# Layer-0 attention with the queries on partitions: a scan over the keys in place of triangular products

## The chip, the cores and the metric

The kernel runs on one core of a Trainium2 chip. The core has five instruction queues: TensorE (PE in the profile; its weight loads are a row of their own, PEld), VectorE (DVE), ScalarE (ACT), GpSimd (POOL) and SyncE (SP, which here issues the weight loads). Each queue runs its instructions in a fixed order; an instruction waits on semaphores for what it reads and for the buffer that it overwrites. The metric is the device time of one execution in microseconds (us); lower is better.

## What is computed

A trunk of two decoder layers over 256 tokens of 1024 features. Layer 0 is stick-breaking attention with 16 heads of 64, then an MLP with squared ReLU; layer 1 is a sparse attention with three branches and a second MLP. Only the attention of layer 0 is touched:

```python
z = jnp.einsum('bqhd,bshd->bhqs', q_blk, k).astype(jnp.float32) * scale
causal = key_pos[None, :] < t[:, None]
log_1m = jnp.where(causal, jax.nn.log_sigmoid(-z), 0.0)
excl = lax.cumsum(log_1m, axis=3, reverse=True) - log_1m
a = jnp.where(causal, jnp.exp(jax.nn.log_sigmoid(z) + excl), 0.0)
return jnp.einsum('bhqs,bshd->bqhd', a.astype(v.dtype), v)
```

With softplus(z) = ln(1 + exp z), log_sigmoid(-z) is -softplus(z) and log_sigmoid(z) is z - softplus(z). So the weight of a key is the exponential of z minus the sum of softplus over this key and all later keys that the query may see. Masked keys count zero in the sum and have weight zero.

## The kernel before

**Weights.** All weights stream through SBUF in pieces of 1 MB in the order of their use. `fetch` (L69) loads a piece on SP, `split` (L79) makes two halves of it: ACT copies a half to `wh` in the reduced format that TensorE multiplies in (L89), DVE subtracts to get the rest, `wl` (L90). Three pieces of each kind fit. Every product with a weight is then three matmuls (`mm3`, L124 to L127): high by high, high by low, low by high. `step` (L100) puts the splitting of a later piece between the matmuls of the present one.

**Attention of layer 0** (`layer0`, L289) works on pairs of heads, p = 0 to 7. Each pair has one row of a piece of `wqk` and goes through four stages:

- `proj(p)` (L345): 48 matmuls of 256 columns give the transposed queries and keys; one DVE multiplication, `qkT` (L354), scales them by the norm of each token.
- `scores(p)` (L357): keys on partitions, queries along the row. Three blocks of 128 x 128 per head: keys 0-127 with all queries, keys 128-255 with the later queries. Two more matmuls add the mask as a bf16 matrix to the diagonal blocks. Softplus is then made on ACT and DVE: absolute value, exponential, logarithm (L373 to L375), and max(z, 0) added (L377). The result is split in two, `sbh` on ACT (L381) and `sbl` on DVE (L382).
- `suffix(p)` (L385): the sum over later keys runs across partitions, so TensorE makes it: products with a triangle of -1 (`tri`) are added to the scores in PSUM, for both parts and both heads, eight matmuls in all. ACT takes the exponential, `sba` (L393), which is the attention weight with keys on partitions, as the next product wants it.
- `values(p)` (L396): weights times values into `po`; `o_evac` (L197) splits the result into `oT_h` on ACT (L198) and `oT_l` on DVE (L199).

The loop (L407 to L414) runs `suffix(p)`, `scores(p+1)`, `values(p)`, `proj(p+2)`. The output projection (`out_proj`, L208) follows, 96 matmuls of 512 columns; the last pair's `suffix` and `values` are hung into it.

**Order of the work.** A planner orders the instructions of each engine when the program is built. In general it follows the order of the program among those that it reckons to be ready; where it reckons a wait, later work moves ahead (the scores of pair 0 stand inside `proj(1)`). Once built, the order is fixed whatever the real durations are.

**PSUM.** Eight banks under two names: four `a` (products of weights, `po`) and four `z` (scores and others). A pair's two score banks are held from `scores` until its exponential in `suffix` has been read, about one period of the loop.

Of the kernel before, what the change touches and what calls it, by code (L numbers as in the profile page):

```python
# [7 lines left out]
F32 = mybir.dt.float32  # L8
# [23 lines left out]
C_ID, C_SB, C_CA, C_TRI, C_ONE, C_CM, C_ANY, C_COS, C_SIN, C_BLK, C_PW, C_END = (  # L32
    0, 128, 256, 384, 512, 640, 670, 672, 704, 736, 740, 744)
# [3 lines left out]
def hybrid_kernel(ctx, tc, x, eye, gcols, gfin, wqk, wv, wo0, wkv, wqa, wqb, wqc, wo1, w1, w2, cw1, cw2, cpos, gate_b, consts, out):  # L37
# [21 lines left out]
    # the weights in the order of their use: loaded ahead, split in two exact parts  # L59
# [19 lines left out]
    def split():  # L79
        """the next half of a piece, split"""  # L80
        j, half = divmod(parts[0], 2)
        parts[0] += 1
        n = stream[j][1]
        if half == 0:
            made.append((wp.tile([P, n], F32R, tag="wh", name="wh", bufs=3),
                         wp.tile([P, n], F32R, tag="wl", name="wl", bufs=3)))
        r = slice(half * n // 2, (half + 1) * n // 2)
        h, lo = made[j]
        nc.scalar.copy(h[:, r], raws[j][:, r])  # L89
        nc.vector.tensor_sub(lo[:, r], raws[j][:, r], f32(h[:, r]))  # L90
        if half:
            fetch()
# [56 lines left out]
    cbf = cp.tile([P, 3 * P], BF16, name="cbf")  # L149
    ident_b, sbm_b, cam_b = cbf[:, 0:P], cbf[:, P:2 * P], cbf[:, 2 * P:3 * P]  # L150
    tri = cp.tile([P, 2 * P], F32R, name="tri")
# [4 lines left out]
    def var_of(parts_):  # L156
        """mean of squares plus eps, per token"""
        ss = sp.tile([P, 2], F32, name="ss")
        for i, src in enumerate(parts_):
            sq = sp.tile([P, D], F32, name="sq", tag="y")  # L160
            tc.keep_in_program_order(
                nc.scalar.activation(sq[:, 0:src.shape[1]], src, AF.Square, accum_out=ss[:, i:i + 1]))
        v = sp.tile([P, 1], F32, name="v", bufs=4)
        if len(parts_) == 2:
            nc.vector.tensor_add(ss[:, 0:1], ss[:, 0:1], ss[:, 1:2])
        nc.vector.tensor_scalar(v, ss[:, 0:1], 1.0 / D, EPS, op0=OP.mult, op1=OP.add)
        return v
# [6 lines left out]
    def xt_tr(half):  # L174
        """four feature blocks of the residual stream, transposed; even blocks in one bank, odd ones in the other"""
        pt = [bank2(f"pt{b}").rearrange("p (j q) -> p j q", j=2) for b in range(2)]
        for b in range(2):
            for j in range(2):
                k = 4 * half + 2 * j + b
                for t in range(T):  # L180
                    nc.tensor.transpose(pt[b][:, j, t * P:(t + 1) * P], hres[t][:, k * P:(k + 1) * P], ident)
        return pt

    def xt_evac(pt, half, gi, xt):
        """times the gain of each feature, split in two"""
# [41 lines left out]
    def mlp(layer, gi, xt, mid, ap):  # L227
        """xt holds the first half of the blocks already; mid runs inside the last products"""
# [60 lines left out]
    def layer0(ap):  # L289
# [33 lines left out]
        nc.gpsimd.tensor_copy(cbf, cst[:, 0:3 * P])  # L323
        nc.gpsimd.tensor_copy(tri, cst[:, C_TRI:C_TRI + 2 * P])
# [32 lines left out]
        def scores(p):  # L357
            qkT = live[p]
            qT, kT = qkT[:, 0, :], qkT[:, 1, :]
            z = [bank2(f"z{hd}") for hd in range(2)]  # L360
            mb = sbm_b[:, None, :].to_broadcast([P, 2, P])
            for hd in range(2):
                r = slice(hd * DH, (hd + 1) * DH)
                mm(z[hd][:, 0:256], kT[r, 0:P], qT[r, :], True, False)
            for hd in range(2):
                r = slice(hd * DH, (hd + 1) * DH)
                mm(z[hd][:, 256:384], kT[r, P:2 * P], qT[r, P:2 * P], False, False)
            for hd in range(2):
                zd = z[hd][:, 0:512].rearrange("p (a q) -> p a q", a=2)[:, :, 0:P]
                mm(zd, ident_b, mb, False, False)  # L370
            na = ap.tile([P, 2, 384], F32, name="na")
            for hd in range(2):
                nc.scalar.activation(na[:, hd, :], z[hd][:, 0:384], AF.Abs)  # L373
            nc.scalar.activation(na, na, AF.Exp, scale=-1.0)
            nc.scalar.activation(na, na, AF.Ln, bias=1.0)  # L375
            for hd in range(2):
                nc.vector.scalar_tensor_tensor(na[:, hd, :], z[hd][:, 0:384], 0.0, na[:, hd, :],  # L377
                                               op0=OP.max, op1=OP.add)
            sh = ap.tile([P, 2, 384], F32R, name="sbh")
            sl = ap.tile([P, 2, 384], F32R, name="sbl")  # L380
            nc.scalar.copy(sh, na)  # L381
            nc.vector.tensor_sub(sl, na, f32(sh))  # L382
            live[p] = z, sh, sl

        def suffix(p):  # L385
            z, sh, sl = live[p]
            for i, a in enumerate((sh, sl)):
                for hd in range(2):
                    mm(z[hd][:, 0:384], tri[:, 0:P], a[:, hd, :], False, False)
                    mm(z[hd][:, P:2 * P], tri[:, P:2 * P], a[:, hd, 256:384], False, i == 1)  # L390
            a = ap.tile([P, 2, 384], F32, name="sba")
            for hd in range(2):
                nc.scalar.activation(a[:, hd, :], z[hd][:, 0:384], AF.Exp)  # L393
            live[p] = a

        def values(p):  # L396
            a = live.pop(p)
            po = bank2("po") if p == NP - 1 else bank("po")
# [11 lines left out]
        for p in range(NP - 1):  # L410
            suffix(p)
            scores(p + 1)
            values(p)
            if p + 2 < NP:  # L414
                proj(p + 2)
        xn = xt_tiles("n")
        out_proj(oT, i_o0, {(0, 0, 3): [lambda: suffix(NP - 1)], (0, 1, 0): [lambda: values(NP - 1)],
# [3 lines left out]
    def nsa(xk, pt0, ap):  # L421
# [47 lines left out]
        def rope(src, t, n):  # L469
            """src[:, h, 0:16] rotated in place; sin holds (-sin, sin), cos (cos, cos)."""  # L470
# [10 lines left out]
        # compressed blocks: windows of the transposed keys and values, plus positions  # L481
# [32 lines left out]
        # keys of the selected and window branches: rotated, transposed, on either half of the partitions, split  # L514
# [37 lines left out]
        # compressed keys and values  # L552
# [114 lines left out]
        # compressed branch: probabilities times gates, transposed, for heads 8 * hf .. 8 * hf + 7  # L667
# [36 lines left out]
        # selected and window branches, and the gated sum of all three  # L704
# [158 lines left out]
def _constants():  # L863
# [4 lines left out]
    c[:, C_SB:C_SB + P] = np.where(i[:, None] < i[None, :], 0.0, NEG)  # L868
    c[:, C_CA:C_CA + P] = np.where(i[None, :] <= i[:, None], 0.0, NEG)
    c[:, C_TRI:C_TRI + P] = np.where(i[:, None] >= i[None, :], -1.0, 0.0)  # L870
    c[:, C_ONE:C_ONE + P] = -1.0
# [17 lines left out]
def _layout(inp):  # L889
# [6 lines left out]
    def blocks(w, nk, cw):  # L896
        """[K, N] -> [N / cw, K / (nk * 128), 128, nk * cw]"""
# [49 lines left out]
```

## Time and profile before

| | us |
|---|---|
| median of 3 runs | 657.2 |
| lowest and highest run | 655.12, 657.46 |
| span of the profiled execution, first to last instruction | 654.1 |
| PE busy | 640.1 (98%) |
| DVE busy | 397.3 (61%) |
| ACT busy | 352.2 (54%) |
| POOL busy | 57.9 (9%) |
| mean granted TensorE clock (share of full speed) | 0.998 |

The profiled execution has its span on record, but no time of its own; the median of the runs is 3.1 us above the span. Times within the trace are counted from the start of the span. Layer 0's attention proper, from the first `qk` product to the first `pu` product of the MLP, runs from 31.3 to 130.1 us. Matmuls are pipelined: one record lasts longer than the distance to the next, so what a matmul costs PE is read from start to start.

### The profile page before, as it was taken

To read this page: it belongs to the slowest core of one execution; us is meant where nothing else is said; L and a number is where in the kernel's file an instruction comes from. 1 tells how busy PE (TensorE), PEld (TensorE's weight loads), DVE (VectorE), ACT (ScalarE), POOL (GpSimd) and SP (SyncE) were. 2 spreads that over 40 slices of the span, in tenths; PEclk is the share of its full clock that TensorE was granted. 3 is DMA by queue.
4 is the path that set the end of the run, shared out by engine and by line. 5 is a ranking of instruction groups with operands and counts; after the bars stand their busy time and mean duration, and the time that the engine had idled before them with its cause. 6 is when DMAs were issued, how large, how long until landed. Compare 5 with 4: busy or idle time off the path is not lost.

```text
span 654.1 us, 10023 instructions
## 1 busy us (share of the span) xinstructions
PE 640.1 (98%) x4096; PEld 563.6 (86%) x4096; DVE 397.3 (61%) x558; ACT 352.2 (54%) x588; POOL 57.9 (9%) x91
## 2 busy tenths in 40 slices
PE   8999999999999999999999999999999999999995
PEld 5899887899999998988888987767998989999994
DVE  5665554675454545555899888773765555454544
ACT  5776676364444444444866767662464454444433
POOL 1000000000000000000133334550000000000000
PEclk9999999999999999999999999999999999999999
DMA  8853332545555554555545750101555555555501
GB/s 325 299 181 126 128 97 98 174 147 193 194 193 194 178 196 164 198 171 187 202 156 177 264 191 2 66 1 63 178 195 180 194 189 193 192 193 193 178 18 64
DMA packets 16894, 106.87 MB, mean 163 GB/s; under 512 B 2256, under 2 KB 2512, under 8 KB 4944
## 3 DMA queue, kind: packets, MB, share of 16 engines
q1 hardware_dynamic: 15696, 104.92, 45.5%
q10 hardware_dynamic: 1152, 1.31, 0.7%
q8 instruction: 32, 0.52, 0.3%
q14 instruction: 14, 0.11, 0.0%
HBM read 105.17 MB, written 1.05 MB: 162 GB/s over the span
## 4 chain that ended last, share of the span: by engine, by line
PE 87%; ACT 4%; DVE 4%; DMA 2%; POOL 2%; issue 1%; SPq 0%; POOLq 0%; ACTq 0%; DVEq 0%
PE acc L125 11%; PE acc L126 11%; PE acc L127 11%; PE pu L126 9%; PE pu L127 9%; PE pu L125 9%; PE po L130 4%; PE qk L125 2%; PE qk L126 2%; ACT wh L89 2%; PE qk L127 2%; PE z L130 2%; PE pk L127 2%; PE pk L126 2%; PE pk L125 2%
## 5 line engine op out<-in xcount | busy, mean ns | idle before, releaser
L90 DVE TENSOR_TENSOR wl<-raw,wh 128x1024 fp32r<-128x1024 f32 (+3 forms) x202 | 237.6, 1200 | 181.5 <-ACT wh L89 181.1
L89 ACT CAST wh<-raw 128x1024 fp32r<-128x1024 f32 (+3 forms) x202 | 200.3, 1023 | 213.1 <-issue 103.8
L126 PE MATMUL pu<-xln,wh 128*128 128x256 f32 x512 | 145.0, 283 | 0.0
L127 PE MATMUL pu<-xhn,wl 128*128 128x256 f32 x512 | 144.9, 283 | 0.0
L125 PE MATMUL pu<-xhn,wh 128*128 128x256 f32 x512 | 144.5, 283 | 0.0
L125 PE MATMUL acc<-wh,hh 128*128 128x512 f32 x256 | 100.0, 392 | 0.0
L126 PE MATMUL acc<-wl,hh 128*128 128x512 f32 x256 | 99.7, 391 | 0.0
L126 PEld LDWEIGHTS pu<-xln,wh 128*128 128x128 f32 x512 | 98.1, 192 | 1.4 <-DVE xln L191 0.2
L127 PE MATMUL acc<-wh,hl 128*128 128x512 f32 x256 | 99.2, 389 | 0.0
L125 PEld LDWEIGHTS pu<-xhn,wh 128*128 128x128 f32 x512 | 98.0, 192 | 1.2
L127 PEld LDWEIGHTS pu<-xhn,wl 128*128 128x128 f32 x512 | 98.1, 192 | 0.0
L127 PEld LDWEIGHTS acc<-wh,hl 128*128 128x128 f32 x256 | 48.1, 188 | 10.5 <-DVE hl L269 0.2
L125 PEld LDWEIGHTS acc<-wh,hh 128*128 128x128 f32 x256 | 48.2, 188 | 9.6 <-ACT hh L268 0.5
L126 PEld LDWEIGHTS acc<-wl,hh 128*128 128x128 f32 x256 | 48.2, 188 | 8.8
L125 PE MATMUL qk<-xha,wh 128*128 128x256 f32 x128 | 36.8, 288 | 0.0
L127 PE MATMUL qk<-xha,wl 128*128 128x256 f32 x128 | 36.3, 283 | 0.0
L126 PE MATMUL qk<-xla,wh 128*128 128x256 f32 x128 | 36.2, 283 | 0.0
L739 POOL TENSOR_TENSOR pe<-pe,rs 128x256 f32<-128x256 f32 (+1 forms) x32 | 26.2, 841 | 25.5 <-DVE rs L735 19.8
L268 ACT CAST hh<-ms 128x512 fp32r<-128x512 f32 x32 | 19.9, 622 | 14.6 <-DVE ms L264 14.6
L699 POOL MEMSET kcb<- 128x120 f32 x1 | 0.2, 200 | 291.1 <-PE acc L127 291.1
L125 PE MATMUL acc<-wh,oT_h 128*128 128x512 f32 x64 | 25.6, 400 | 0.0
L125 PEld LDWEIGHTS qk<-xha,wh 128*128 128x128 f32 x128 | 24.5, 191 | 1.1 <-issue 1.0
(188 smaller groups left out, 972.3 us busy)
## 6 DMA issues: line engine op xcount, KB each, us to landing
raw<-in_w SPq DMA_DIRECT2D x64, 1024.0 KB, 4.8
raw<-in_wqk SPq DMA_DIRECT2D x8, 1024.0 KB, 4.9
raw<-in_wo SPq DMA_DIRECT2D x8, 1024.0 KB, 4.8
raw<-in_wkv SPq DMA_DIRECT2D x6, 1024.0 KB, 5.0
raw<-in_cw SPq DMA_DIRECT2D x4, 1024.0 KB, 5.1
raw<-in_wv SPq DMA_DIRECT2D x3, 1024.0 KB, 7.1
raw<-in_wqb SPq DMA_DIRECT2D x2, 768.0 KB, 4.2
raw<-in_wqc SPq DMA_DIRECT2D x2, 768.0 KB, 5.2
```

What stands on the lines that cost most here:

```text
L89: nc.scalar.copy(h[:, r], raws[j][:, r])
L90: nc.vector.tensor_sub(lo[:, r], raws[j][:, r], f32(h[:, r]))
L125: nc.tensor.matmul(o, a[0], b[0], start=first, stop=False, skip_group_check=True)
L126: nc.tensor.matmul(o, a[0], b[1], start=False, stop=False, skip_group_check=True)
L127: nc.tensor.matmul(o, a[1], b[0], start=False, stop=last, skip_group_check=True)
L130: nc.tensor.matmul(o, a, b, start=first, stop=last, skip_group_check=True)
L268: nc.scalar.copy(hh, sv)
L699: nc.gpsimd.memset(kcb, 0.0)
L739: nc.gpsimd.tensor_tensor(s, s, rs[:, t, :][:, :, None].to_broadcast([P, 2, n]), op=OP.mult)
```

## The change

The scores are made with the queries on partitions and the keys along the row. The sum over later keys is then a sum along the row, which one DVE instruction, a scan from the last key to the first, makes for both heads at once. The row of a head has three segments of 128 scores, each followed by one column that holds -1e30 (`SEG` = 129, `ROW` = 387). The factor `go_on` is 1 except at two such columns, where it is 0 and restarts the sum.

The mask is a minimum with a constant, 40 or -1e30, taken by DVE when it reads the scores out of PSUM. Softplus is made directly as ln(1 + exp z), so the absolute value, the maximum and the split in two are gone. The weights come out with queries on partitions and have to be turned: a new stage `turn(p)` transposes six blocks on TensorE and copies them out of PSUM, one head on ACT and one on DVE. The loop runs one pair further ahead: the scores of pair p+2 are made while pair p is turned.

```diff
-    ident_b, sbm_b, cam_b = cbf[:, 0:P], cbf[:, P:2 * P], cbf[:, 2 * P:3 * P]
-    tri = cp.tile([P, 2 * P], F32R, name="tri")
+    ident_b, cam_b = cbf[:, 0:P], cbf[:, P:2 * P]
...
-        nc.gpsimd.tensor_copy(cbf, cst[:, 0:3 * P])
-        nc.gpsimd.tensor_copy(tri, cst[:, C_TRI:C_TRI + 2 * P])
+        nc.gpsimd.tensor_copy(cbf, cst[:, 0:2 * P])
+
+        go_on = ap.tile([P, 2 * ROW], BF16, name="go_on", bufs=1)
+        nc.gpsimd.memset(go_on, 1.0)
+        nc.gpsimd.memset(go_on.rearrange("p (h c) -> p h c", h=2)[:, :, 2 * SEG - 1:ROW:SEG], 0.0)
...
         def scores(p):
...
-                mm(z[hd][:, 0:256], kT[r, 0:P], qT[r, :], True, False)
+                mm(z[hd][:, 0:256], qT[r, P:2 * P], kT[r, :], True, False)
...
-                mm(z[hd][:, 256:384], kT[r, P:2 * P], qT[r, P:2 * P], False, False)
+                mm(z[hd][:, 256:384], qT[r, 0:P], kT[r, 0:P], False, True)
+            e = ap.tile([P, 2 * ROW], F32, name="sbe", bufs=3)
+            nc.gpsimd.memset(e.rearrange("p (b c) -> p b c", b=6)[:, :, P:SEG], NEG)
+            cap = cst[:, C_CAP:C_CAP + 3 * P].rearrange("p (b c) -> p b c", b=3)
             for hd in range(2):
-                zd = z[hd][:, 0:512].rearrange("p (a q) -> p a q", a=2)[:, :, 0:P]
-                mm(zd, ident_b, mb, False, False)
-            na = ap.tile([P, 2, 384], F32, name="na")
+                nc.vector.tensor_tensor(
+                    e[:, hd * ROW:(hd + 1) * ROW].rearrange("p (b c) -> p b c", b=3)[:, :, 0:P],
+                    z[hd][:, 0:384].rearrange("p (b c) -> p b c", b=3), cap, op=OP.min)
+            s = ap.tile([P, 2 * ROW], F32, name="sbs", bufs=2)
+            nc.scalar.activation(s, e, AF.Exp)
+            nc.scalar.activation(s, s, AF.Ln, bias=1.0)
+            nc.vector.tensor_tensor_scan(s[:, ::-1], s[:, ::-1], go_on[:, ::-1], 0.0, OP.add, OP.mult)
+            nc.vector.tensor_sub(e, e, s)
+            nc.scalar.activation(e, e, AF.Exp)
+            live[p] = e
+
+        def turn(p):
+            e = live[p]
+            at = ap.tile([P, 2, 384], F32, name="sbt")
             for hd in range(2):
-                nc.scalar.activation(na[:, hd, :], z[hd][:, 0:384], AF.Abs)
-            nc.scalar.activation(na, na, AF.Exp, scale=-1.0)
-            nc.scalar.activation(na, na, AF.Ln, bias=1.0)
...
-        def suffix(p):
...
+                pt = bank2("pa")
+                for i, b in enumerate((2, 0, 1)):
+                    c = hd * ROW + b * SEG
+                    nc.tensor.transpose(pt[:, i * P:(i + 1) * P], e[:, c:c + P], ident)
+                if hd:
+                    nc.vector.tensor_copy(at[:, hd, :], pt[:, 0:384])
+                else:
+                    nc.scalar.copy(at[:, hd, :], pt[:, 0:384])
+            live[p] = at

         def values(p):
             a = live.pop(p)
-            po = bank2("po") if p == NP - 1 else bank("po")
+            po = bank2("po") if p >= NP - 2 else bank("po")
...
         proj(1)
-        for p in range(NP - 1):
-            suffix(p)
-            scores(p + 1)
+        scores(1)
+        for p in range(NP - 2):
+            proj(p + 2)
+            turn(p)
+            scores(p + 2)
             values(p)
-            if p + 2 < NP:
-                proj(p + 2)
         xn = xt_tiles("n")
-        out_proj(oT, i_o0, {(0, 0, 3): [lambda: suffix(NP - 1)], (0, 1, 0): [lambda: values(NP - 1)],
+        out_proj(oT, i_o0, {(0, 0, 1): [lambda: turn(NP - 2)], (0, 0, 2): [lambda: values(NP - 2)],
+                            (0, 1, 2): [lambda: turn(NP - 1)], (0, 1, 3): [lambda: values(NP - 1)],
                             (1, 1, 2): [lambda: xt_evac(xt_tr(0), 0, 1, xn)]})
```

The table of constants keeps its size: the two mask and triangle blocks give way to the 384 columns of `cap`.

More of the change, by code (lines that the diff above doesn't have):

```diff
@@ L30 @@
 GELU_C = 2.0 * 0.7978845608028654
-C_ID, C_SB, C_CA, C_TRI, C_ONE, C_CM, C_ANY, C_COS, C_SIN, C_BLK, C_PW, C_END = (
-    0, 128, 256, 384, 512, 640, 670, 672, 704, 736, 740, 744)
+C_ID, C_CA, C_CAP, C_CM, C_ANY, C_COS, C_SIN, C_BLK, C_PW, C_END = (
+    0, 128, 256, 640, 670, 672, 704, 736, 740, 744)
+SEG = P + 1
+ROW = 3 * SEG
 @with_exitstack
@@ L148, in hybrid_kernel @@
     cst = cp.tile([P, C_END], F32, name="cst")
-    cbf = cp.tile([P, 3 * P], BF16, name="cbf")
-    ident_b, sbm_b, cam_b = cbf[:, 0:P], cbf[:, P:2 * P], cbf[:, 2 * P:3 * P]
-    tri = cp.tile([P, 2 * P], F32R, name="tri")
+    cbf = cp.tile([P, 2 * P], BF16, name="cbf")
+    ident_b, cam_b = cbf[:, 0:P], cbf[:, P:2 * P]
     ident_r = cp.tile([P, P], F32R, name="ident_r")
@@ L360, in scores @@
             z = [bank2(f"z{hd}") for hd in range(2)]
-            mb = sbm_b[:, None, :].to_broadcast([P, 2, P])
             for hd in range(2):
                 r = slice(hd * DH, (hd + 1) * DH)
-                mm(z[hd][:, 0:256], kT[r, 0:P], qT[r, :], True, False)
+                mm(z[hd][:, 0:256], qT[r, P:2 * P], kT[r, :], True, False)
             for hd in range(2):
                 r = slice(hd * DH, (hd + 1) * DH)
-                mm(z[hd][:, 256:384], kT[r, P:2 * P], qT[r, P:2 * P], False, False)
+                mm(z[hd][:, 256:384], qT[r, 0:P], kT[r, 0:P], False, True)
@@ L374, in scores @@
-            nc.scalar.activation(na, na, AF.Exp, scale=-1.0)
[L375 to L382, printed above, removed]
@@ L383, in scores @@
-            live[p] = z, sh, sl
-        def suffix(p):
[L386 to L394, printed above, removed]
+                nc.vector.tensor_tensor(
+                    e[:, hd * ROW:(hd + 1) * ROW].rearrange("p (b c) -> p b c", b=3)[:, :, 0:P],
+                    z[hd][:, 0:384].rearrange("p (b c) -> p b c", b=3), cap, op=OP.min)
@@ L867, in _constants @@
     c[:, C_ID:C_ID + P] = np.eye(P)
-    c[:, C_SB:C_SB + P] = np.where(i[:, None] < i[None, :], 0.0, NEG)
     c[:, C_CA:C_CA + P] = np.where(i[None, :] <= i[:, None], 0.0, NEG)
-    c[:, C_TRI:C_TRI + P] = np.where(i[:, None] >= i[None, :], -1.0, 0.0)
-    c[:, C_ONE:C_ONE + P] = -1.0
+    c[:, C_CAP:C_CAP + P] = 40.0
+    for b in (1, 2):
+        c[:, C_CAP + b * P:C_CAP + (b + 1) * P] = np.where(i[None, :] < i[:, None], 40.0, NEG)
     inv = np.float32(500000.0) ** (-np.arange(8, dtype=np.float32) * np.float32(2.0) / np.float32(16))
```

## The prediction

> **What bounds the kernel now.** I read the page first, its busy times and the chain that ended last:
>
> ```profile
> PE 640.1 (98%) x4096; PEld 563.6 (86%) x4096; DVE 397.3 (61%) x558; ACT 352.2 (54%) x588; POOL 57.9 (9%) x91
> PE 87%; ACT 4%; DVE 4%; DMA 2%; POOL 2%; issue 1%; SPq 0%; POOLq 0%; ACTq 0%; DVEq 0%
> ```
>
> TensorE is the bound of the whole and 87% of the chain. Whether that holds in the stage that changes, and in the one that inherits the gain, is in the stretches view (length, then busy us and instructions of PE, PEld, DVE, ACT, POOL, then clock, DMA share, GB/s): two periods of the loop of layer 0, and a piece of the MLP.
>
> ```profile
> 63.07:72.61 9.54, 9.46 (x76) 8.40 (x75) 5.46 (x7) 6.32 (x10) 0.00 (x0) 1.00 0.34 110
> ...
> 91.69:101.23 9.54, 9.46 (x76) 8.40 (x75) 5.46 (x7) 6.32 (x10) 0.00 (x0) 1.00 0.33 110
> ...
> 200.00:250.00 50.00, 50.00 (x315) 45.39 (x314) 27.25 (x28) 23.03 (x29) 0.00 (x0) 1.00 0.52 180
> ```
>
> Every period is 9.54 us, to the end of the loop. PE has no gap to speak of; DVE (5.46) and ACT (6.32) have room. The MLP behind is PE without a pause with DMA half used, so what layer 0 gives up in time on PE arrives at the end whole. Next I read PE's timeline over one period, start, length, instruction:
>
> ```profile
> 62.95 0.28 PE L127 MATMUL qk<-xha,wl 128*128 128x256 f32 x1
> 63.07 0.68 PE L130 MATMUL z<-sbh,tri 128*128 128x384 f32 x4
> 63.59 0.73 PE L130 MATMUL z<-sbl,tri 128*128 128x384 f32 x4
> 64.26 0.92 PE L130 MATMUL z<-qkT 64*128 64x256 f32 x8
> 65.11 0.39 PE L130 MATMUL z<-cbf 128*128 128x256 bf16 x2
> 65.59 1.25 PE L130 MATMUL po<-sba,v 128*64 128x256 f32 x8
> 66.76 0.39 PE L125 MATMUL qk<-xha,wh 128*128 128x256 f32 x1
> 66.98 0.28 PE L126 MATMUL qk<-xla,wh 128*128 128x256 f32 x1
> ...
> 65.58 0.19 PEld L130 LDWEIGHTS po<-sba,v 128*64 128x64 f32 x2 [0.36 <-ACT sba L393]
> 65.97 0.62 PEld L130 LDWEIGHTS po<-sba,v 128*64 128x64 f32 x6 [0.19 <-ACT sba L393]
> ```
>
> From start to start: triangular products 1.19 (63.07 to 64.26), scores 0.85, mask 0.48, values 1.17, together 3.69 us; the rest of the period, 5.85, is the 48 products of `proj`. The last two rows are weight loads: the values wait on the exponential `sba`, 0.36 before the first head and 0.19 before the second. The first of these lies within the mask's 0.48, the second within the values' 1.17. In the first period, with `sba` ready earlier, the same eight products took 0.85:
>
> ```profile
> 46.84 0.92 PE L130 MATMUL po<-sba,v 128*64 128x256 f32 x8
> 47.69 0.39 PE L125 MATMUL qk<-xha,wh 128*128 128x256 f32 x1
> ```
>
> **The change, part by part.** *PE.* Gone from each pair: 1.19 of triangular products, the mask, and the waits on `sba`. The scores keep their shapes (64 rows by 256 and by 128 columns), 0.85. New are six transposes. The sparse attention has transposes of the same shape and type; the six that start at 419.19 show the price:
>
> ```profile
> 419.19 0.27 PE L748 MATMUL ptp<-ident,pe 128*128 128x128 f32 x1
> ...
> 419.74 0.27 PE L750 MATMUL ptp<-ident,pe 128*128 128x128 f32 x1
> 419.77 0.71 PE L130 MATMUL z<-kT,qs 128*128 128x512 f32 x2
> ```
>
> Five steps in 0.55 us, 0.11 each: 0.66 for six.
>
> *Two waits.* The scores wait for the multiplication `qkT`, on DVE. The DVE and ACT timelines of the same period:
>
> ```profile
> 63.27 0.69 DVE L354 TENSOR_TENSOR qkT<-qk,rbq 128x512 f32<-128x512 f32 x1 [0.97 <-PE qk L127]
> 64.23 2.36 DVE L90 TENSOR_TENSOR wl<-raw,wh 128x1024 fp32r<-128x1024 f32 x2 [0.27 <-ACT wh L89]
> 67.27 0.42 DVE L199 TENSOR_TENSOR oT_l<-po,oT_h 128x256 fp32r<-128x256 f32 x1 [0.68 <-ACT oT_h L198]
> 68.90 1.02 DVE L377 SCALAR_TENSOR_TENSOR na<-z,na 128x384 f32<-128x384 f32 x2 [1.20 <-ACT na L375]
> 70.88 0.96 DVE L382 TENSOR_TENSOR sbl<-na,sbh 128x768 fp32r<-128x768 f32 x1 [0.95 <-ACT sbh L381]
> ...
> 63.15 1.99 ACT L89 CAST wh<-raw 128x1024 fp32r<-128x1024 f32 x2 [1.84 <-PE qk L126]
> 65.05 0.86 ACT L393 ACTIVATE sba<-z 128x384 f32<-128x384 f32 x2
> 68.02 0.85 ACT L375 ACTIVATE na<-na 128x768 f32<-128x768 f32 x1
> ```
>
> The multiplication ends 0.89 after the section starts (63.07 to 63.96). Today 1.19 of triangular products cover it; 0.66 of transposes don't. With 0.06 for the signal the scores start at 0.95: an exposed wait of 0.29. Between nothing (the planner fills it with the next `proj`, as it did for pair 0) and more (something ahead of the multiplication on DVE), I take 0.29.
>
> The values now wait for two copies out of PSUM. Rows of their shape in the sparse attention:
>
> ```profile
> L752 DVE COPY pT<-ptp 128x384 f32<-128x384 f32 x24 | 12.8, 548 | 6.4 <-PE ptp L750 6.3
> L754 ACT COPY pT<-ptp 128x384 f32<-128x384 f32 x8 | 3.9, 493 | 0.2 <-PE ptp L750 0.2
> ```
>
> On ACT the copy can stand between the two halves of the split: ready at about 0.5, the first half ends at 1.08, the copy at 1.57. On DVE it follows the multiplication, 0.89 to 1.44. The scores end at 1.80, so both hide. If one `wl` (half of 2.36, 1.18) stands ahead of the DVE copy, the second head waits to about 2.7. So it costs 0 to 1.2; I take 0.19, the nearest row (the second head's wait today).
>
> A section of the loop is then 0.66 + 0.29 + 0.85 + 0.85 + 0.19 = 2.84 instead of 3.69, the period 8.69.
>
> *DVE.* Off its 5.46 come the maximum (1.02) and `sbl` (0.96); on it come two minima out of PSUM (the same form as the maximum, 1.02), the subtraction (0.97, as `sbl`), the copy (0.55): 6.02 without the scan. No row shows a scan over 774 elements. From below: a two-input instruction over 768 takes 0.96. From above: the slowest per element is the reciprocal,
>
> ```profile
> L733 DVE RECIPROCAL rs<-rs 128x4 f32<-128x4 f32 x16 | 2.6, 164 | 0.7 <-ACT pe L727 0.7
> L600 DVE RECIPROCAL gates<-gates 128x48 f32<-128x48 f32 x2 | 0.9, 442 | 0.0
> ```
>
> (442 - 164) / 44 = 6.3 ns an element, so 774 would take 5.0 us. I take 0.97, being nearest to the two-input row in inputs, type and length: DVE is busy 6.99 of 8.69. After the scores the chain is two minima, exponential, logarithm, scan, subtraction, exponential: 1.02 + 0.85 + 0.85 + 0.97 + 0.97 + 0.85 = 5.5, and its result is wanted two periods on. But the next multiplication `qkT` stands behind the subtraction in DVE's queue. With one `wl` ahead of the minima (1.44 to 2.62), they end near 3.65, the logarithm at 5.4, the scan at 6.4, the subtraction at 7.4; the multiplication is wanted at 8.9. So 1.5 us of room.
>
> [...]
>
> *ACT.* Gone: two absolute values, `sbh`, two `sba`; added: one exponential of 774 and one copy, so 6.32 - 0.87 - 0.83 - 0.86 + 0.85 + 0.49 = 5.1. No bound.
>
> *POOL.* Before the loop the `tri` cast goes and two fills come; in the loop six columns are filled per pair.
>
> ```profile
> 14.07 1.39 POOL L324 CAST tri<-cst 128x256 fp32r<-128x256 f32 x1
> 15.42 1.19 POOL L326 CAST cmb<-cst 128x30 bf16<-128x30 f32 x1
> 19.73 0.55 POOL L171 TENSOR_TENSOR r<-v,cst 128x1 f32<-128x1 f32 x1 [3.12 <-DVE v L166]
> L699 POOL MEMSET kcb<- 128x120 f32 x1 | 0.2, 200 | 291.1 <-PE acc L127 291.1
> ```
>
> At 200 ns for 120 columns, 774 cost at most 1.3, about what the cast cost, with 3.12 us of idle time behind. The fill in the loop, some 0.2, meets an idle POOL, and its buffer (three) comes free long before. Nothing. No DMA moves; SP's queue is passed by nothing. Score banks are released sooner.
>
> *Sum over the layer.* Before: seven sections of 3.69 (p = 0 to 6); 0.97 for pair 0's scores and mask (0.85, and 0.48 less the wait of 0.36); 2.24 in the output projection, 1.19 + 0.85 and two changes of weight form at 0.1 (the step from 66.76 to 66.98 is 0.22, where two `qk` products otherwise lie 0.12 apart): together 29.0. After: six sections of 2.84, two early `scores` of 0.95, and twice 0.66 + 0.85 + 0.2 in the output projection: 17.0 + 1.9 + 3.4 = 22.3. The last pair's chain of 5.5 hides behind the first 36 products of the projection, 0.23 from start to start:
>
> ```profile
> 105.72 0.40 PE L125 MATMUL acc<-wh,oT_h 128*128 128x512 f32 x1
> 105.95 0.39 PE L126 MATMUL acc<-wl,oT_h 128*128 128x512 f32 x1
> ```
>
> That is 8.3 us of cover. So 6.7 us less: span 647.4. The median stands 3.1 above the span, so **650.5 us**. Without the two waits (6 x 0.48) it would be 647.6.
>
> **The rivals.** *A, the forecast*: 647 to 653.9. *B, the waits eat it*: DVE's fixed order puts a `wl` ahead of the copy, or the scan takes more than the 2.5 us that the room allows, so that `qkT` comes late; PE stands 1.0 to 1.3 longer per section, about one `wl`. Six sections lose 6 x 1.0 to 6 x 1.3 = 6 to 8: 656.5 to 658.5. For it: DVE goes from 5.46 of 9.54 to at least 6.99 of 8.69, and the order is fixed ahead of durations that it may have wrong. Against: the room above, and that ready work of an earlier stage goes first. *C, DVE becomes the bound; slower*: with the scan at the reciprocal's rate DVE needs 6.02 + 5.0 = 11.0 per period; 6 x (11.0 - 9.54) = 8.8, less 1.6 saved outside the loop: about 664.4. It decides from a scan of 9.54 - 6.02 = 3.5 us; between 2.5 and 3.5 it takes gain away. Against: no other two-input row is nearly so slow. *D, the gain doesn't reach the end*, because the weight stream limits the MLP: 657. Against: the MLP's stretch.
>
> **How the numbers follow.** A 0.61, B 0.26 (a `wl` in the wrong place is enough), C 0.10, D 0.03. Half a per cent, 3.3 us, is what a measurement here can tell from no change: 653.9 to 660.5. A falls below it. Of B I give 0.03 to slower, when both orders go wrong at once, and 0.23 to the same. So faster 0.61, the same 0.26, slower 0.13. The range goes from 646.0, a little under the sum without waits, to 659.5, over B; outside are C and the ends of A and B.
>
> **What would show it.** The period of the loop, 8.69; six transposes at 0.11; a gap before the scores near 0.29; no wait of the values on the DVE copy over 0.5; the scan near 0.97 us and DVE near 6.99 a period. Wrong it would be if the scan takes over 2.5, or the values or scores wait behind `wl`, the scan or the subtraction for a microsecond per pair.

## The result and the profile after

| | before | after |
|---|---|---|
| median of 5 runs, us | 656.99 (654.94 to 657.46) | 651.29 (650.93 to 652.83) |
| span of the profiled execution, us | 654.1 | 649.3 |
| time of the profiled execution, us | not recorded | 651.07 |

The ratio is 0.9927 [0.9910, 0.9944]: faster by 0.7%. The forecast was 650.5. The span fell by 4.8 us; the sum had 6.7. Runs of one kernel spread with their mean granted clock (the changed kernel took 650.93 us at 0.999 and 652.83 at 0.992), and the profiled executions of four kernels below were at 0.991 to 0.996, so stretches of the profiles are compared beside the times.

First the page of the changed kernel, its busy times and the chain that ended last:

```profile
PE 631.3 (97%) x4064; PEld 557.1 (86%) x4064; DVE 413.2 (64%) x574; ACT 343.0 (53%) x564; POOL 57.5 (9%) x100
PE 84%; DVE 7%; ACT 3%; issue 2%; POOL 2%; DMA 1%; POOLq 0%; SPq 0%; DVEq 0%; ACTq 0%
```

TensorE still sets the whole, but DVE has gone from 4 to 7% of the chain. Where DVE ended up on the path is the question of this section. The stretches view of the changed kernel, a period of the loop and a piece of the MLP:

```profile
78.92:87.63 8.71, 8.39 (x72) 7.60 (x71) 7.57 (x9) 5.18 (x8) 0.11 (x1) 1.00 0.32 122
...
200.00:250.00 50.00, 50.00 (x333) 46.17 (x332) 26.04 (x26) 22.31 (x26) 0.00 (x0) 1.00 0.52 189
```

The period is 8.71 (forecast 8.69). DVE is busy for 7.57 of it (forecast 6.99, with a scan of 0.97). The MLP is TensorE without a pause, as before.

PE's timeline of the changed kernel through one section of the loop, `turn`, `scores`, `values` and the next `proj`:

```profile
78.92 0.82 PE L396 MATMUL pa<-ident,sbe 128*128 128x128 f32 x6
...
79.87 0.92 PE L133 MATMUL z<-qkT 64*128 64x256 f32 x8
...
80.98 0.87 PE L133 MATMUL po<-sbt,v 128*64 128x256 f32 x8 [0.19 <-ACT sbt L400]
...
81.78 0.39 PE L128 MATMUL qk<-xha,wh 128*128 128x256 f32 x1
```

From start to start: 0.95 for the transposes with the wait on `qkT`, 1.11 for the scores and a wait, 0.80 for the values: 2.86, forecast 2.84. The wait before the values is on ACT's copy (`sbt`, L400), which the forecast had ready in time. DVE's and ACT's timelines show why:

```profile
75.89 1.77 DVE L384 TENSOR_TENSOR_SCAN sbs<-sbs,go_on 128x774 f32<-128x774 f32 x1 [0.41 <-ACT sbs L383]
77.77 0.97 DVE L385 TENSOR_TENSOR sbe<-sbe,sbs 128x774 f32<-128x774 f32 x1
79.12 0.69 DVE L359 TENSOR_TENSOR qkT<-qk,rbq 128x512 f32<-128x512 f32 x1 [0.39 <-PE qk L130]
79.78 0.56 DVE L398 COPY sbt<-pa 128x384 f32<-128x384 f32 x1
```

```profile
78.77 0.85 ACT L386 ACTIVATE sbe<-sbe 128x774 f32<-128x774 f32 x1 [2.90 <-DVE sbe L385]
79.52 1.03 ACT L92 CAST wh<-raw 128x1024 fp32r<-128x1024 f32 x1
80.46 0.47 ACT L400 COPY sbt<-pa 128x384 f32<-128x384 f32 x1
```

The scan takes 1.77 us. `qkT` is not delayed by it: DVE waits 0.39 for the last `qk` product first. But the last exponential of the chain can only start at 78.77, when scan and subtraction are done. In ACT's order a half of the weight split stands behind it, and the copy behind that: it ends at 80.93, and the values start at 80.98.

The time that is missing against the sum is at the start of the loop. The view of PE's waits in the changed kernel, from the first queries and keys of pair 0 to the MLP (total us, times, longest):

```profile
PE z L133 <- DVE qkT L359: 2.6, 2, 1.5
PE po L133 <- ACT sbt L400: 0.6, 3, 0.2
```

(The 0.2 of the second line counts from the end of the record before; from start to start the wait is 0.26.) Two waits on `qkT` make 2.6 us, both before the steady periods. PE's timeline has them, the scores of pairs 1 and 2, and DVE's shows what stood ahead:

```profile
46.45 0.92 PE L133 MATMUL z<-qkT 64*128 64x256 f32 x8 [1.12 <-DVE qkT L359]
...
53.80 0.92 PE L133 MATMUL z<-qkT 64*128 64x256 f32 x8 [1.50 <-DVE qkT L359]
```

```profile
37.86 2.36 DVE L93 TENSOR_TENSOR wl<-raw,wh 128x1024 fp32r<-128x1024 f32 x2 [0.27 <-ACT wh L92]
40.13 1.02 DVE L378 TENSOR_TENSOR sbe<-z,cst 128x384 f32<-128x384 f32 x2
43.02 1.77 DVE L384 TENSOR_TENSOR_SCAN sbs<-sbs,go_on 128x774 f32<-128x774 f32 x1 [1.87 <-ACT sbs L383]
44.83 0.96 DVE L385 TENSOR_TENSOR sbe<-sbe,sbs 128x774 f32<-128x774 f32 x1
45.71 0.68 DVE L359 TENSOR_TENSOR qkT<-qk,rbq 128x512 f32<-128x512 f32 x1
...
51.40 1.77 DVE L384 TENSOR_TENSOR_SCAN sbs<-sbs,go_on 128x774 f32<-128x774 f32 x1 [1.80 <-ACT sbs L383]
53.09 0.66 DVE L359 TENSOR_TENSOR qkT<-qk,rbq 128x512 f32<-128x512 f32 x1
```

The multiplication of pair 1 stands behind pair 0's whole chain, with two `wl` at its head (37.86 to 40.13), and that of pair 2 behind pair 1's scan. In both cases DVE itself stood still for 1.8 us in front of the scan, waiting for the logarithm. `qkT` could not have filled these pauses: counted at 48 products a pair, the last `qk` product of pair 1 starts at 43.37, and that of pair 2 is this one on PE's timeline:

```profile
51.36 0.28 PE L130 MATMUL qk<-xha,wl 128*128 128x256 f32 x1
```

Both end after the pause (43.65 and 51.64, the pauses at 43.02 and 51.40). What `qkT` waits for is the scan (for pair 1 the subtraction too), which starts so late that it fills DVE just when the multiplication becomes ready.

### The profile page after: what moved, and what is told of

Its sections match the earlier page's. It is cut to its first block, busy times and chain, and to the rows that moved or that the text cites. A ratio compares the mean times of both kernels' runs of the same rounds, so it can differ in the third digit from the quotient of the medians.

```text
span 649.3 us, 9971 instructions
## 1 busy us (share of the span) xinstructions
PE 631.3 (97%) x4064; PEld 557.1 (86%) x4064; DVE 413.2 (64%) x574; ACT 343.0 (53%) x564; POOL 57.5 (9%) x100
## 3 DMA queue, kind: packets, MB, share of 16 engines
q1 hardware_dynamic: 15696, 104.92, 44.1%
HBM read 105.17 MB, written 1.05 MB: 164 GB/s over the span
## 4 chain that ended last, share of the span: by engine, by line
PE 84%; DVE 7%; ACT 3%; issue 2%; POOL 2%; DMA 1%; POOLq 0%; SPq 0%; DVEq 0%; ACTq 0%
PE acc L128 11%; PE acc L129 11%; PE acc L130 11%; PE pu L129 10%; PE pu L130 9%; PE pu L128 9%; PE po L133 3%; PE pk L130 2%; PE pk L129 2%; PE pk L128 2%; DVE wl L93 2%; DVE sbs L384 1%; PE pv L128 1%; PE pv L129 1%; PE pv L130 1%
## 5 line engine op out<-in xcount | busy, mean ns | idle before, releaser
L130 PE MATMUL acc<-wh,oT_l 128*128 128x512 f32 x64 | 25.0, 391 | 0.0
```

Source lines behind the costliest of these rows:

```text
L130: nc.tensor.matmul(o, a[1], b[0], start=False, stop=last, skip_group_check=True)
```

## The experiments

The theory: TensorE sets the pace of the loop; what the change loses against the sum is the scan's length, on DVE's fixed order at the start and by way of ACT in the steady periods. The rivals: DVE's load, rather than its order, is the loss; running two pairs ahead does nothing; or the mask, and not the sum over keys, brings the gain. Each time is the median of 4 to 6 runs, beside the kernel before on the same chip (655.99, 655.73 and 655.84 us on the three chips).

Two stretches sort all runs. The loop is the time from the first product of pair 0's `proj` to the first product of the output projection, the tail from there to the first product of the MLP, both between starts on PE's timeline in each profile. For the changed kernel the three starts are 30.94, 99.21 and 125.48, in the kernel before 31.31, 104.92 and 130.13.

| kernel | loop, us | tail, us | time, us | ratio to before |
|---|---|---|---|---|
| before | 73.61 | 25.21 | 656.99 | |
| after | 68.27 | 26.27 | 651.29 | 0.9927 [0.9910, 0.9944] |
| changed_again | 68.29 | 26.27 | 651.49 | 0.9934 [0.9920, 0.9947] |
| scan_gone | 65.69 | 26.25 | 648.60 | 0.9887 [0.9874, 0.9899] |
| scan_twice | 77.25 | 26.26 | 661.65 | 1.0081 [1.0068, 1.0094] |
| early_proj | 67.14 | 26.27 | 649.75 | 0.9904 [0.9892, 0.9917] |
| early_again | 67.13 | 26.27 | 650.24 | 0.9911 [0.9897, 0.9925] |
| turn_inside | 68.38 | 27.57 | 652.92 | 0.9955 [0.9943, 0.9967] |
| values_later | 68.49 | 26.61 | 651.95 | 0.9952 [0.9939, 0.9964] |
| mask_mm | 69.18 | 27.42 | 653.53 | 0.9967 [0.9955, 0.9980] |
| one_ahead | 73.87 | 26.81 | 657.79 | 1.0033 [1.0021, 1.0044] |
| pool_only | 67.90 | 26.26 | 652.15 | 0.9937 [0.9922, 0.9951] |
| pool_early | 66.97 | 26.27 | 649.92 | 0.9904 [0.9890, 0.9917] |
| pool_later | 68.68 | 26.27 | 652.56 | 0.9953 [0.9934, 0.9972] |

**scan_gone: an elementwise product in the scan's place.** The sum over later keys is left out; everything else stays.

```diff
-            nc.vector.tensor_tensor_scan(s[:, ::-1], s[:, ::-1], go_on[:, ::-1], 0.0, OP.add, OP.mult)
+            nc.vector.tensor_tensor(s, s, go_on, op=OP.mult)
```

> The scan is replaced by one elementwise multiplication over the same 774 columns; the sum over later keys is left out. In the changed kernel the scan takes 1.76 us and the multiplication should take 0.97, so DVE has 0.8 us less per pair, some 7.0 of the 8.72 us period. Theory: in the steady loop PE sets the pace, so the period stays at 8.72 within 0.05; only the two waits of PE on qkT at the start of the loop (1.12 and 1.50 us in the changed kernel) shrink, by about 0.8 each, and the time falls by 1 to 2 us, to about 649.7. Rival: the scan, and with it DVE, already limits the steady loop; then the period falls by 0.3 to 0.8 us and the time by 3 to 6 us, to 645 to 648.

The groups view of this kernel (61 to 96 us) has the price of what stands there now, and the view of PE's waits what is left of them:

```profile
L384 DVE TENSOR_TENSOR sbs<-sbs,go_on 128x774 f32<-128x774 f32 x4 | 3.9, 967 | 1.6 <-ACT sbs L383 1.6
```

```profile
PE z L133 <- DVE qkT L359: 1.0, 2, 0.7
```

The product takes 0.967 us, just the price that the prediction gave the scan. So this run is the forecast kernel with the forecast's price, and the loop is 2.6 shorter than in the changed kernel. The two waits at the start fall from 2.6 to 1.0. The wait on ACT's copy is gone, and the period is 8.45 instead of 8.71:

```profile
77.05:85.50 8.45, 8.32 (x72) 7.60 (x71) 6.67 (x9) 5.30 (x7) 0.11 (x1) 1.00 0.33 124
```

ACT's timeline shows the reason: the exponential starts at 76.01, 1.04 us before its section (77.05); in the changed kernel it starts 0.15 before (78.77 and 78.92). So the weight half is through earlier, and the copy with it: it ends 1.50 us after the start of the section, where the changed kernel's ends after 2.01.

```profile
76.01 0.85 ACT L386 ACTIVATE sbe<-sbe 128x774 f32<-128x774 f32 x1 [2.10 <-DVE sbe L385]
77.13 1.05 ACT L92 CAST wh<-raw 128x1024 fp32r<-128x1024 f32 x1 [0.27 <-PE qk L129]
78.08 0.47 ACT L400 COPY sbt<-pa 128x384 f32<-128x384 f32 x1
```

Four sections of the changed kernel have that wait (from pair 2 on): 4 x 0.26 = 1.0, with the 1.6 at the start 2.6, which is the whole difference. The scan's extra 0.8 us costs 2.6 us of loop; 1.0 of waiting at the start is left without it. By DVE's timeline that is the place in the queue; no run moves it there. Neither expectation held: the theory had the period unchanged, the rival had it fall by 0.3 or more and the time to 648 or less; the measured 0.26 and 648.60 lie between. The way through ACT was seen only in this trace.

**scan_twice: a second scan of the same length into a scratch tile.**

```diff
+            x = ap.tile([P, 2 * ROW], F32, name="sbx", bufs=1)
+            nc.vector.tensor_tensor_scan(x, s, go_on, 0.0, OP.add, OP.mult)
             nc.vector.tensor_sub(e, e, s)
```

> A second scan of 774 columns per pair into a scratch tile that nothing reads; the result is as before it. DVE's busy time per pair goes from about 7.8 to about 9.55 us, over the 8.72 us period. Theory (DVE is the next bound, with about 0.9 us to spare per period): the period goes to 9.5 to 9.7 us, six periods lose about 5, and with the longer waits at the start of the loop the time is 656 to 659, the gain of the change gone. Rival (the cost of the scan is hidden whatever it is, since PE paces the loop): the period stays at 8.72 and the time near 651.

The time is 661.65, slower than before and above what was expected. The stretches view of two periods, the first from `qkT` to `qkT`, the second from scores to scores, and PE's waits:

```profile
76.54:85.98 9.44, 8.32 (x70) 7.61 (x70) 9.00 (x11) 4.24 (x6) 0.02 (x1) 1.00 0.31 113
...
86.92:97.22 10.30, 8.40 (x71) 7.61 (x71) 9.08 (x11) 5.18 (x8) 0.11 (x1) 1.00 0.26 102
```

```profile
PE z L133 <- DVE qkT L359: 8.5, 6, 1.8
```

TensorE waits for `qkT` before the scores of pair 1 and in five of the six sections, and the kernel is slower than before at 2 x 1.77 = 3.54 us of scan, the point from which rival C of the prediction was to decide. But it is not DVE's load alone: 9.44 is one of the short periods, and in the last two, of 10.30 and 10.31, DVE stands idle for 1.2 us, waiting for ACT's halves of the split and for the logarithm. So the longer chain, here too, takes more than DVE's work.

**early_proj: `proj(2)` ahead of `scores(1)`,** so that the first wait has 5.85 us of products to hide behind.

```diff
         proj(1)
+        proj(2)
         scores(1)
         for p in range(NP - 2):
-            proj(p + 2)
+            if p:
+                proj(p + 2)
             turn(p)
```

> The products of proj(2) are moved ahead of scores(1), so that PE has work while qkT of pair 1 is still behind the scan and the subtraction of pair 0 on DVE. Theory (the two waits of 1.12 and 1.50 us at the start are what is missing from the forecast gain): the wait of 1.12 goes, that of 1.50 shrinks or goes, the time falls by 1.1 to 2.6 us, to 648.7 to 650.2, with the period unchanged at 8.72. Rival (the waits only move: each pair's scores come later, and the pair after waits instead): within 0.5 us of the changed kernel.

```profile
PE po L133 <- ACT sbt L400: 1.1, 5, 0.3
PE z L133 <- ACT sbt L400: 0.7, 1, 0.7
PE pa L396 <- ACT sbe L386: 0.3, 1, 0.3
```

The view of PE's waits no longer names `qkT`. All waits together fall from 3.2 to 2.1, and the loop by 1.13; the rest moved to other steps of the first two sections. The same kernel on another chip:

> early_proj once more, beside the next three on one chip: 649.7 us within 0.6.

The loop is 67.13 against 67.14, the time 650.24. Against the lower of the two medians of the changed kernel, 651.29, that is 1.5 and 1.1 us less. The intervals of the ratios overlap, so the times alone don't settle it; the loops agree to 0.02 us between two profiles of the same kernel (changed and changed_again, early_proj and early_again) and differ by 1.1 between the kernels. Among the versions that compute everything early_proj is, with pool_early below, the best, and ahead of both kernels.

**turn_inside: `turn(p)` between the products of `proj(p+2)`, `values(p)` before `scores(p+2)`,** to hide the copies.

```diff
-        def proj(p):
+        def proj(p, mid=None):
...
+                if k == 5 and mid is not None:
+                    mid()
...
-            proj(p + 2)
-            turn(p)
-            scores(p + 2)
+            proj(p + 2, lambda: turn(p))
             values(p)
+            scores(p + 2)
```

> turn(p) stands inside proj(p+2), before its last nine products, and values(p) before scores(p+2). The copies out of PSUM and the multiplication qkT are then covered by other products of PE. Theory (per period PE waits 0.29 us on qkT and 0.26 on the ACT copy, and nothing else limits the loop): the period falls from 8.72 to about 8.25, six periods give 2.5 to 3 us, the time is about 648.5. Rival (DVE at 7.8 us of queue work per period cannot follow 8.25, its order makes qkT late): the waits grow elsewhere, the period stays within 0.15 of 8.72 and the time within 1 us of the changed kernel.

DVE's timeline in this kernel (its lines are two higher, the scan is L386), and the weight loads of the values:

```profile
86.68 1.77 DVE L386 TENSOR_TENSOR_SCAN sbs<-sbs,go_on 128x774 f32<-128x774 f32 x1 [0.73 <-ACT sbs L385]
88.36 0.53 DVE L400 COPY sbt<-pa 128x384 f32<-128x384 f32 x1
88.81 0.95 DVE L387 TENSOR_TENSOR sbe<-sbe,sbs 128x774 f32<-128x774 f32 x1
89.68 0.68 DVE L361 TENSOR_TENSOR qkT<-qk,rbq 128x512 f32<-128x512 f32 x1
...
88.95 0.62 PEld L133 LDWEIGHTS po<-sbt,v 128*64 128x64 f32 x6 [0.43 <-DVE sbt L400]
```

Scan, copy and subtraction run one behind the other. The period, from the `qkT` before at 80.39, is 9.29 instead of 8.71, and what TensorE pays is mostly the copy, which now stands behind the scan: the values take 1.42 (88.33 to 89.75) instead of 0.80, while the late `qkT` costs 0.17 of waiting. The loop as a whole only seems to come out even (68.38): the scores of pair 7 stand at 99.72, behind the first product of the output projection (99.04), so they count in the tail, which grows by 1.3. Loop and tail together are 95.95, in the changed kernel 94.54. Neither expectation had this: a period of 8.25 or one within 0.15 of 8.72.

**values_later: `values` a section later,** with early_proj's start, so that the copies have a period.

```diff
+        turn(0)
+        scores(2)
+        for p in range(1, NP - 2):
             proj(p + 2)
             turn(p)
+            values(p - 1)
             scores(p + 2)
-            values(p)
+        values(NP - 3)
```

> As early_proj, and in the loop values(p-1) stands between turn(p) and scores(p+2), so that both waits of PE in a period (0.29 on qkT, 0.26 on the ACT copy) have 0.85 us of other products in front of them. DVE has the same work, 7.6 us. Theory (PE paces the loop, and the two waits are all that stands between 8.72 and the products alone): the period falls to 8.15 to 8.25, five periods give 2.5 us on top of what early_proj gave, the time is 647 to 648. Rival (DVE's fixed order has no room below 8.7, as when turn stood inside proj): qkT comes later, the period stays between 8.6 and 9.3, the time at 649.5 or above.

The loop is 68.49, 1.35 above early_proj's. From transposes to transposes the periods are 8.29, 8.25 and 8.43 (from 61.85 to 86.82), close to the theory's, and then one of 10.37 gives it all back: in it PE has a wait of 2.05 us on `qkT`, ahead of the scores at 90.49. DVE's timeline before it:

```profile
81.31 2.55 DVE L93 TENSOR_TENSOR wl<-raw,wh 128x1024 fp32r<-128x1024 f32 x2 [0.79 <-ACT wh L92]
...
84.12 1.01 DVE L378 TENSOR_TENSOR sbe<-z,cst 128x384 f32<-128x384 f32 x2
87.00 1.77 DVE L384 TENSOR_TENSOR_SCAN sbs<-sbs,go_on 128x774 f32<-128x774 f32 x1 [1.86 <-ACT sbs L383]
...
89.75 0.68 DVE L359 TENSOR_TENSOR qkT<-qk,rbq 128x512 f32<-128x512 f32 x1
```

It is the picture of the start of the loop once more: two `wl` ahead of the minima, a pause of 1.86 for the logarithm, and `qkT` right behind the subtraction. In the periods that keep to the theory one `wl` stands ahead of the minima and the other behind them, and the scan waits 0.73.

**mask_mm: the mask by two bf16 products on TensorE again;** DVE copies the scores out of PSUM without a minimum.

```diff
-                mm(z[hd][:, 256:384], qT[r, 0:P], kT[r, 0:P], False, True)
+                mm(z[hd][:, 256:384], qT[r, 0:P], kT[r, 0:P], False, False)
+            mb = sbm_b[:, None, :].to_broadcast([P, 2, P])
+            for hd in range(2):
+                mm(z[hd][:, P:3 * P].rearrange("p (b c) -> p b c", b=2), ident_b, mb, False, True)
...
-                nc.vector.tensor_tensor(
+                nc.vector.tensor_copy(
                     e[:, hd * ROW:(hd + 1) * ROW].rearrange("p (b c) -> p b c", b=3)[:, :, 0:P],
-                    z[hd][:, 0:384].rearrange("p (b c) -> p b c", b=3), cap, op=OP.min)
+                    z[hd][:, 0:384].rearrange("p (b c) -> p b c", b=3))
```

> One part of the change undone: the mask is again two bf16 products added to the scores in PSUM, and DVE only copies the scores out. Theory (a product costs the loop what it costs PE): two products of 256 columns add some 0.24 to 0.35 us to each period, which goes to 9.0 to 9.05, and the time is 2 to 3 us longer than the changed kernel, 653 to 654. Rival (PE's waits absorb them): within 0.7 us of the changed kernel.

The changed kernel beside it on the same chip:

> The changed kernel once more, beside the next three on one chip: 651.3 us within 0.6, period 8.72.

The mask on TensorE costs 2.0 us (653.53 against 651.49). The period hardly pays: 8.78 (transposes at 80.08 and, a period on, 88.86) instead of 8.71. PE's timeline of mask_mm:

```profile
81.88 0.39 PE L133 MATMUL z<-cbf 128*128 128x256 bf16 x2
82.20 0.87 PE L133 MATMUL po<-sbt,v 128*64 128x256 f32 x8
```

The two products take 0.32, and no wait is left before the values: the mask stands in the 0.26 in which the changed kernel waited for ACT's copy. So the time lies where the theory put it (2 to 3 us more), but not for its reason, a period of 9.0. The loop is 0.9 longer. The tail grows by 1.15. There the weights of pair 6 come late: their products reach from 104.23 to 106.24, 2.01 where the changed kernel has 0.87, with a wait of 0.51 on DVE's copy. In DVE's order that copy stands behind a scan:

```profile
103.11 1.77 DVE L386 TENSOR_TENSOR_SCAN sbs<-sbs,go_on 128x774 f32<-128x774 f32 x1 [0.39 <-ACT sbs L385]
104.80 0.53 DVE L400 COPY sbt<-pa 128x384 f32<-128x384 f32 x1
```

In the changed kernel it stands ahead of it (101.56 and 102.04). By these lines the tail's part comes from another order on DVE, and not from what the mask costs TensorE.

**one_ahead: the loop of before, one pair ahead,** with the new arithmetic.

```diff
-        scores(1)
-        for p in range(NP - 2):
-            proj(p + 2)
+        for p in range(NP - 1):
             turn(p)
-            scores(p + 2)
+            scores(p + 1)
             values(p)
+            if p + 2 < NP:
+                proj(p + 2)
```

> One part of the change undone: the loop runs turn(p), scores(p+1), values(p), proj(p+2) again, one pair ahead and not two, with the last pair's turn and values where its suffix and values stood. Theory: the chain from the scores to the last exponential, 1.0 + 0.85 + 0.85 + 1.76 + 0.97 + 0.85 with its signals about 6.6 us, now has only values and proj to hide in, 0.85 + 5.85; with a wl ahead of it in DVE's queue turn waits 0.5 to 1.5 us in each period, the period is 9.2 to 10 and the time 654 to 660. Rival (running ahead is worth nothing, PE still has its work ready): the period stays at 8.7 and the time within 1 us of the changed kernel, or under it by the 2.6 us of waits at the start.

The last pair alone is then hung into the output projection. The time is 657.79, 6.3 above changed_again on the same chip and 0.3% above the kernel before. The view of PE's waits over loop and tail:

```profile
PE pa L396 <- ACT sbe L386: 7.5, 7, 3.1
```

All of it is on the chain's last exponential. With one pair ahead the chain from scores to exponential doesn't fit beside one `proj`; the period is 9.18 (83.85 to 93.03), at the lower end of what the theory had. Of the 5.6 us that the loop is longer, 1.5 may belong to this execution alone: in its first section the scores and values take 1.59 and 1.54 instead of 0.85 and 0.80 (the mean granted clock of the execution was 0.991, of changed_again's 0.998). The lowest of its runs is 656.56 us, still above the kernel before.

**pool_only: half of the weight rests on POOL** during `proj(2)` to `proj(7)`, so that DVE has less to do.

```diff
-        nc.vector.tensor_sub(lo[:, r], raws[j][:, r], f32(h[:, r]))
+        (nc.gpsimd if half == 1 and relief[0] else nc.vector).tensor_sub(lo[:, r], raws[j][:, r], f32(h[:, r]))
...
         scores(1)
+        relief[0] = True
         for p in range(NP - 2):
...
+        relief[0] = False
         xn = xt_tiles("n")
```

> The changed kernel, with one of the two wl subtractions of each pair from proj(2) to proj(7) moved from DVE to POOL, which is idle there. By the rate of POOL's multiplications in the sparse attention (1069 ns for 512 columns, 613 for 256) it takes about 2.0 us; nothing waits for it for a whole period. DVE falls from 7.6 to about 6.4 us per period; PE's products stay as they are. Theory (the scan is paid for through the fixed order of DVE and ACT, as scan_gone showed with 8.45): the scan ends about 1 us earlier, so the last exponential is out of the way of the ACT copy, the period falls from 8.72 to about 8.45 and the time by 1.5 to 2.5 us, to 649 to 650. Rival (what scan_gone gained was the length of the chain, which this doesn't shorten): the period stays at 8.72, the time within 0.6 us of the changed kernel.

The stretches view of this kernel, one period from the exponential ahead of a section to the next, and a part of DVE's timeline (lines are one higher):

```profile
80.11:88.82 8.71, 8.40 (x72) 7.60 (x72) 6.43 (x8) 5.19 (x8) 2.52 (x2) 1.00 0.36 121
```

```profile
85.85 1.77 DVE L385 TENSOR_TENSOR_SCAN sbs<-sbs,go_on 128x774 f32<-128x774 f32 x1 [1.53 <-ACT sbs L384]
```

DVE is busy 6.43, 1.14 less, and the period is the same 8.71, as the rival had it. The scan only waits longer for its input, 1.53 instead of 0.41: it is the length of the chain that counts in the steady periods, not the load of DVE as such. The `wl` that moved had stood between the minima and the scan, where DVE waits for ACT anyway. The other one stayed ahead of the minima, which start at 82.97, 0.9 after the scores end (82.04); moving that one may shorten the chain by as much, and was not tried. (The layer's first product comes at 32.55 in this profile, 1.6 later than in the changed kernel, before anything that was edited. The mean granted clock of this execution was 0.996, of the changed kernel's 0.998; the layer starts as late, at 32.67 and 32.56, in the profiled executions of scan_twice (0.992) and values_later (0.996). The two lowest of its runs, 651.08 and 651.24, are as fast as the changed kernel's.)

The same edit with early_proj's, and with values_later's:

> early_proj and pool_only together. If the gains add (1.5 us at the start of the loop, 0.27 per period): 647.5 to 648.5, period 8.45. If DVE and POOL hinder each other, with DVE's instructions longer than 1.77 for the scan and 0.97 for the subtraction: at or above early_proj.

> values_later, with one wl subtraction of each pair on POOL. values_later failed at 651.95 with qkT late by up to 2 us behind the scan and the subtraction. Theory (DVE's room was what it lacked): with 1.2 us less on DVE qkT comes in time, PE has both waits covered, the period is 8.15 to 8.25 and the time 646.5 to 648. Rival (the chain through ACT and DVE takes its time whatever DVE's load): waits on qkT or on the last exponential stay, the period is 8.5 or more, the time above 648.5.

pool_early, at 649.92, is early_proj again: the gains do not add, and the scan keeps its 1.77. In pool_later (652.56) the period is 9.04, with DVE busy for 6.29 of it:

```profile
77.60:86.64 9.04, 8.32 (x72) 7.62 (x70) 6.29 (x10) 5.08 (x7) 2.51 (x2) 1.00 0.33 115
```

DVE idles for 2.75 us of each period and TensorE still waits for `qkT` (4.5 us in five waits, by the view of PE's waits). An engine with nearly a third of its time free can be the one that sets the pace, if what is wanted from it stands behind a chain that passes through another engine.

Not tried: a program in which `qkT` stands ahead of the scan in DVE's order at the start, which is where the 1.0 us that scan_gone still waits for could be had.

## Why the prediction was right, and which term was off

**The bound and the way to the end: right.** The gain is made in the loop (73.61 to 68.27, 5.3 less), the tail gives 1.06 back (forecast 3.4 - 2.24 = 1.2), and what is behind shifts whole: the MLP starts 4.65 earlier (0.37 of it because the layer's first product does, 30.94 against 31.31) and the span ends 4.8 earlier. Rival D is out.

**The section of the loop: right in sum, in part by luck.** Transposes and the wait on `qkT` 0.95 (0.66 + 0.29), section 2.86 (2.84), period 8.71 (8.69). The wait on `qkT` came out with the size and the cause that were forecast. The wait of 0.19 did not: at the scan's forecast price it isn't there (scan_gone, section 2.60, period 8.45). A scan taken too short and a wait that belongs to the longer scan met in the sum.

**The second wait: near in size by luck, wrong in cause.** I had put 0.19 on DVE's copy and hidden ACT's. DVE's copy ends at 80.34, before the scores do; it is ACT's that comes last, by 0.26, because the late exponential and a weight half stand ahead of it. "On ACT the copy can stand between the two halves of the split" overlooked the exponential, and its place depends on the scan.

**The scan: the term that was mis-sized.** I took 0.97 as "nearest to the two-input row in inputs, type and length"; it measures 1.77, inside the bounds of 0.97 and 5.0. The room of 1.5 us for `qkT` was worked out for a steady period, where it holds (DVE still waits 0.39 for the last `qk` product before `qkT`), and not for the start, nor for ACT. scan_gone, which puts exactly 0.97 in its place, has a loop of 65.69, 7.92 less than before; the steps of the sum for the loop are 29.0 - 2.24 less 22.3 - 3.4, 7.86. That they agree to 0.1 is luck again. In scan_gone five sections take 2.60 instead of 2.84, 1.2 less in all, and the start takes 1.2 more: 0.3 for the scores of pair 1 and 0.8 in the first section (50.62 to 54.28, 3.66).

**The start of the loop: missed.** "Two early `scores` of 0.95" allowed 0.1 each beside the 0.85 of the products, and no wait on `qkT`. In the changed kernel the waits on `qkT` are 1.12 for pair 1 and 1.50 for pair 2. That is rival B's mechanism, in two places instead of six. For 1.6 of the 2.6 the scan's length is the cause (scan_gone). The other 1.0 is put down to the place behind the chain, which the pause for the logarithm makes late; that is read from DVE's timeline and not shown by a run of its own, though both waits on `qkT` vanish when `proj(2)` goes ahead (early_proj).

**From span to time: two errors that met.** I set the median 3.1 above the span, from a profile without a time of its own. The profiled execution after took 651.07 for a span of 649.3, 1.8 around it. The span came out 1.9 above the forecast, this 1.3 below. Without the second error the forecast would have been about 649.2, and still inside the range.

**DVE's and POOL's share: right that neither is a bound.** DVE is busy for 7.57 of 8.71, 0.58 above the forecast 6.99, and is no bound with one scan of 1.77; to be slower than before takes two (scan_twice), and even there DVE idles for up to 1.2 us of a period. POOL's fill in the loop takes 0.11 and hides.

**What the change owes to its parts.** The mask's move is worth 2.0 us of the 4.2 that changed_again gains on the same chip (655.73 to 651.49); but 1.15 of it lies in the tail, where one copy stands in another place of DVE's order (mask_mm), so 0.9 is what the loop shows. And the whole pays only with two pairs ahead: one pair ahead gives all of it back (one_ahead).

## What to carry to other kernels

When work is moved from the busiest engine to one with room, compare not the busy times but the chain that the work becomes a link of, and work out the first rounds of a loop by themselves: there nothing runs ahead yet, and a late link of the chain stands in the in-order queue just when the next pair's work becomes ready. A price that is bounded by a factor of five should be followed through every queue that it stands in, at both ends; here 0.8 us more of one instruction cost nothing where the room had been looked for, and 2.6 us in two places where it had not.

## What the runs showed of the hardware

The sum took the scan at the price of a two-input instruction. Over the same 128 x 774 the groups view of the changed kernel (61 to 130 us) has

```profile
L384 DVE TENSOR_TENSOR_SCAN sbs<-sbs,go_on 128x774 f32<-128x774 f32 x5 | 8.8, 1770 | 1.6 <-ACT sbs L383 1.6
L385 DVE TENSOR_TENSOR sbe<-sbe,sbs 128x774 f32<-128x774 f32 x6 | 5.8, 966 | 0.6
```

so (1770 - 966) / 774 = 1.04 ns more for each column. From 512 to 768 columns the two-input rows grow by (0.96 - 0.69) / 256 = 1.05 ns a column: at this one length the scan costs as if it paid for each column twice. Neither the reversed reading nor the bf16 factor is what costs: the product of scan_gone reads the same factor and takes 0.967, and the second scan of scan_twice runs forward and takes as long:

```profile
74.20 1.77 DVE L386 TENSOR_TENSOR_SCAN sbx<-sbs,go_on 128x774 f32<-128x774 f32 x1
```

In pool_only the half of the weight rest that POOL makes takes about twice as long as DVE's 1.22 us:

```profile
L94 POOL TENSOR_TENSOR wl<-raw,wh 128x1024 fp32r<-128x1024 f32 x6 | 14.6, 2438 | 34.6 <-ACT wh L93 29.2 <-DVE wl L94 3.4 <-PE po L134 2.1
```

In the four of these halves from 57.12 us on DVE ran only the two minima and the `oT_l` subtraction beside it, which take what they take in the changed kernel (1.01 to 1.02, and 0.41); whether its other instructions would be slower beside POOL isn't shown.
